# Gate units of a streaming encoder layer: sigmoids and stores put off to later places in the order

## The chip, the core and the metric

The kernel runs on one core of one Trainium2 chip, in one launch. The metric is device time in microseconds, the median of several runs; lower is better. Five engines run their own instruction streams: TensorE (PE, with PEld for its weight loads), VectorE (DVE), ScalarE (ACT), GpSimd (POOL) and SyncE (SP), which here only issues DMAs. An engine works through its own stream in order and waits at an instruction until the data and the buffers that it needs are there.

## The reference

One layer over 1024 frames of width 1024, in float32. What the change touches is the gates: two 1024 x 1024 slices of `w_in` give logits, and their sigmoids scale two mixer branches much later.

```python
h = rmsnorm(x, norm_mix_g[li])
z = h @ w_in[li]
qa, fa, ia, ga, qb, kb, vb, gate_a, gate_b = jnp.split(z, split_at, axis=-1)
...
merged = (jax.nn.sigmoid(gate_a) * (oa @ w_branch_a[li])
          + jax.nn.sigmoid(gate_b) * (ob @ w_branch_b[li]))
x = x + merged @ w_out[li]
```

The rest (the HGRN2 mixer, banded attention, SwiGLU, the per-layer embedding) is as long as the layer but is not edited.

## The kernel before

Activations lie feature-major, 128 partitions by 1024 frames. Each float32 matmul is made of three single-pass ones: both operands are split into a rounded part and a remainder (`whi` and `wlo` for weights), and hi x hi, hi x lo and lo x hi are summed in PSUM. ScalarE makes the rounded part (a CAST), VectorE or GpSimd the remainder.

**Gate units.** 14 of the 16 gate tiles are made in `gate_units` by 7 units, n = 0 to 6, of two output tiles (c = 0, 1) by two halves of the frames. A unit is one Strassen-like step (`strassen`, L1282): 7 products in place of 8, each of 4 chunks of the contraction by 3 matmuls, 12 matmuls of 128x512. From n = 1 on the products run in the order 0 to 6 into three PSUM banks:

- product 0 into b1; ScalarE copies b1 to the tile p1 (the **copy**, `self.A.copy(p1, b1)`)
- product 1 into b2; VectorE adds u2 = p1 + b2
- product 2 into b3
- product 3 on top of b2, which is why it waits for u2; VectorE adds u3 = p1 + b2 + b3, and `done(1, 0, u3)`
- product 4 on top of b1; `done(0, 1, b1)`
- product 5 on top of b2; `done(1, 1, p1 + b2)`
- product 6 on top of b3; u2 += b3 and `done(0, 0, u2)`

Unit 0 (`early`) runs its products in the order 0, 4, 6, 1, 2, 3, 5 and has other places for the four results. `done` is `keep` of `gate_units`: VectorE multiplies the result by the row norms `rb`, ScalarE takes the sigmoid in place, SyncE stores the 256 KB half to DRAM. The result tiles `t` come from a pool of five (`stmp`), so a tile is used again once its store has landed.

**Side work.** `strassen` pulls a generator `side()` after the copy, at five places between the products and at the end. Three things come from it:

- `gate_load`: two weight loads of 512 KB (`wr`) for the next unit. The raw tiles are two, so a load waits until GpSimd has made the last remainders from the old ones.
- `first_weights` (L1077): the next unit's operands from the four quarters of its weights: casts of the first and of the last two quarters with GpSimd's remainders; three **weight sums** by VectorE in place; casts of two sums with VectorE's remainders; a cast and remainder of the third; a last sum, cast and remainder.
- from n = 1 on `quad_item` (L923): a 1 MB load `dq` of weights for a much later product, four **dq sums** by VectorE in place, four stores. It has one buffer, so the next load waits for these stores to land.

**What sets the order.** The code pins the stream of VectorE, ScalarE, GpSimd, TensorE and SyncE to the order in which the Python code emits the instructions (`order`, through `self.V`, `self.A`, `self.G`, `load`, `store`). No scheduler moves them in this stage. Behind the units comes `near(0)`, where GpSimd (L470) makes remainders in tiles that lie where the dq buffer lay, and TensorE multiplies them by `onesr`.

Of the kernel before, what the change touches and what calls it, by code (L numbers as in the profile page):

```python
# [13 lines left out]
AF = mybir.ActivationFunctionType  # L14
# [40 lines left out]
class Trunk:  # L55
# [296 lines left out]
    def gate_units(self, first, then):  # L352

        h0, h1 = slice(0, HALF), slice(HALF, T)
        cut = lambda pair, h: [t[:, h] for t in pair]
        odd, even = self.u[1::2], self.u[0::2]
        self.sops = [
            [cut(p, h1) for p in odd], [cut(a, h1) for a, _ in self.ts], [cut(b, h0) for _, b in self.ts],
            [cut(a, h0) for a, _ in self.ts], [cut(p, h1) for p in even], [cut(b, h1) for _, b in self.ts], [cut(p, h0) for p in even]]
        self.gd = [self.spill() for _ in range(2 * GATES)]  # L360

        for n in range(GATES):
            def keep(c, half, ps):
                hs = slice(half * HALF, half * HALF + HALF)
                t = self.stmp() if n and (c, half) == (0, 1) else ps
                self.V.tensor_tensor(t, ps, self.rb[:, hs], ALU.mult)
                self.A.activation(t, t, AF.Sigmoid)
                self.store(self.gd[2 * n + c][:, hs], t)

            def side():  # L370
                more, item = iter(()), iter(())
                if n + 1 < GATES:
                    self.gate_load()
                    more = self.first_weights()
                else:
                    then()
                if n:
                    item = self.quad_item(1, 0)
                    next(item)
                yield  # L380
                yield
                next(more, None)
                next(more, None)
                yield
                next(item, None)
                next(item, None)
                next(more, None)
                yield
                next(more, None)
                next(item, None)  # L390
                yield
                drain(more)
                drain(item)

            self.strassen(keep, side(), early=n == 0)


    def hgrn_in(self, h, outs=None, first=None):
# [1298 lines left out]
def drain(stream):  # L1697
    while True:
        try:
            next(stream)  # L1700
        except StopIteration as e:
            return e.value
# [114 lines left out]
```

## Time and profile before

| | |
|---|---|
| median of 3 runs | 1654.88 us (1654.5 to 1656.84) |
| span of the profiled execution | 1655.2 us |
| PE busy | 1597.5 us, 97% |
| DVE busy | 1190.9 us, 72% |
| POOL busy | 702.9 us, 42% |
| ACT busy | 618.6 us, 37% |
| DMA, mean over the span | 123 GB/s |
| mean granted TensorE clock | 0.985 |

Busy shares are means over stages with different limits. The gate units lie between about 75 and 230 us of the span. In a timeline row stand the start, the duration, the engine, the line, the operation, the tiles written and read (without their numbers), the shape, and in brackets how long the engine had been idle and who ended that. Nearly all rows of this stage bear the line of a helper that records the order (L52, L76, L81), so they are told apart by their tiles: `pm` is a PSUM bank, `t` a result tile, `wr` raw weights, `d` a DRAM tile. Rows of SPq are DMA issues; where several are merged, the duration runs from the first to the last.

### The profile page before, as it was taken

The numbers are of one execution on the slowest core, as the hardware profiler recorded it, in microseconds if no ns is written. First come the engines' busy times: TensorE is split into PE (matmuls) and PEld (weight loads), VectorE is DVE, ScalarE is ACT, GpSimd is POOL, SyncE is SP. The second block draws the span as 40 slices with busy tenths as digits, with TensorE's granted clock in tenths as the row PEclk, the third lists the DMA queues.
The fourth block names the chain that finished last, engine by engine and source line by source line (L and its number), as shares of the span: only waits on it lengthen the run. The fifth ranks groups of instructions, "written<-read, shape, count | busy, mean of one in ns | idle before, by whom it ended". The sixth has DMA issues, their size and how long they took to land.

```text
span 1655.2 us, 22544 instructions
## 1 busy us (share of the span) xinstructions
PE 1597.5 (97%) x8656; PEld 1351.9 (82%) x8656; DVE 1190.9 (72%) x1838; ACT 618.6 (37%) x1080; POOL 702.9 (42%) x408
## 2 busy tenths in 40 slices
PE   6988889999999999999898999999999999999998
PEld 5876769898989999878686788888888888888887
DVE  8755667676648888756988798888888866446653
ACT  5422232122117777631365532222222234435421
POOL 2222342232134322213523377777776665545420
PEclk9999999999999999999999999999999999999999
DMA  4025551211010110087534432233332268655521
GB/s 184 27 101 191 197 184 65 89 39 47 30 62 16 43 43 35 14 317 273 197 127 165 148 101 96 95 104 100 110 113 96 70 220 317 220 190 185 197 76 52
DMA packets 70524, 204.36 MB, mean 123 GB/s; under 512 B 7952, under 2 KB 8720, under 8 KB 68496
## 3 DMA queue, kind: packets, MB, share of 16 engines
q1 hardware_dynamic: 70272, 202.90, 35.0%
q8 instruction: 68, 1.11, 0.3%
q14 instruction: 40, 0.33, 0.1%
q10 hardware_dynamic: 144, 0.02, 0.0%
HBM read 147.05 MB, written 55.84 MB: 123 GB/s over the span
## 4 chain that ended last, share of the span: by engine, by line
PE 43%; DVE 5%; DMA 1%; ACT 1%; issue 1%; POOL 1%; SPq 0%; DVEq 0%; ACTq 0%
PE pm L81 43%; DVE s L52 4%; ACT s L52 1%; POOL wl L124 1%; DMA wr<-in_sg 0%; DMA wr<-d 0%; DMA wr<-in_su 0%; DVE q L52 0%; DMA wr<-in_pp 0%; ACT wh L121 0%; DVE wl L124 0%; ACT q L52 0%; ACT whi L52 0%; DVE wr L52 0%; POOL s L840 0%
## 5 line engine op out<-in xcount | busy, mean ns | idle before, releaser
L81 PE MATMUL pm<-s,wh 128*128 128x512 f32 (+1 forms) x1688 | 525.3, 392 | 16.6 <-DVE s L52 10.7
L81 PE MATMUL pm<-s,whi 128*128 128x512 f32 x1568 | 494.6, 397 | 9.1 <-ACT whi L52 3.5
L124 POOL TENSOR_TENSOR wl<-wr,wh 128x1024 fp32r<-128x1024 f32 (+2 forms) x100 | 251.6, 2521 | 367.6 <-ACT wh L121 362.0
L81 PEld LDWEIGHTS pm<-s,wh 128*128 128x128 f32 x1688 | 316.3, 189 | 84.1 <-DVE s L52 12.9
L81 PEld LDWEIGHTS pm<-s,whi 128*128 128x128 f32 x1568 | 298.2, 190 | 78.3 <-ACT whi L52 3.9
L81 PE MATMUL pm<-s,wl 128*128 128x512 f32 (+1 forms) x844 | 329.4, 390 | 0.0
L81 PE MATMUL pm<-s,wlo 128*128 128x512 f32 x784 | 310.4, 396 | 0.0
L52 DVE TENSOR_TENSOR s<-s,s 128x512 f32<-128x512 f32 (+3 forms) x202 | 251.0, 1269 | 75.2 <-ACT s L52 41.6
L81 PE MATMUL pm<-wh,s 128*128 128x256 f32 (+1 forms) x1152 | 252.3, 304 | 0.1
L121 ACT CAST wh<-wr 128x1024 fp32r<-128x1024 f32 (+2 forms) x106 | 106.4, 1005 | 292.8 <-PE pm L81 126.2
L52 POOL TENSOR_TENSOR wlo<-wr,whi 128x512 fp32r<-128x512 f32 x74 | 139.1, 1889 | 149.7 <-ACT whi L52 149.0
L81 PEld LDWEIGHTS pm<-wh,s 128*128 128x128 f32 x1152 | 191.5, 192 | 5.5 <-DVE s L52 0.3
L81 PEld LDWEIGHTS pm<-s,wl 128*128 128x128 f32 x844 | 159.7, 189 | 33.0 <-POOL wl L124 0.5
L81 PEld LDWEIGHTS pm<-s,wlo 128*128 128x128 f32 x784 | 149.1, 190 | 34.3 <-DVE wlo L52 0.5
L81 PE MATMUL pm<-wl,s 128*128 128x256 f32 (+1 forms) x576 | 170.6, 296 | 0.0
L52 DVE TENSOR_TENSOR t<-pm,t 128x512 f32<-128x512 f32 x143 | 98.2, 687 | 86.5 <-PE pm L81 76.0
L52 POOL TENSOR_TENSOR s<-s,t 128x512 f32<-128x512 f32 x44 | 76.5, 1739 | 90.0 <-ACT t L52 90.0
L81 PEld LDWEIGHTS pm<-wl,s 128*128 128x128 f32 x576 | 111.0, 193 | 2.1
L52 DVE TENSOR_TENSOR s<-pm,s 128x512 f32<-128x512 f32 x101 | 65.3, 684 | 61.9 <-PE pm L81 61.9
L52 ACT CAST whi<-q 128x512 fp32r<-128x512 f32 (+1 forms) x63 | 47.8, 759 | 156.5 <-DVE q L52 134.5
L81 PE MATMUL pm<-s,s 128*128 128x64 f32 (+4 forms) x776 | 98.3, 267 | 1.9 <-DVE s L52 1.7
L81 PEld LDWEIGHTS pm<-s,s 128*128 128x128 f32 (+2 forms) x776 | 86.5, 174 | 7.4 <-DVE s L52 3.6
(141 smaller groups left out, 1940.8 us busy)
## 6 DMA issues: line engine op xcount, KB each, us to landing
s<-d SPq DMA_DIRECT2D x65, 512.0 KB, 5.9
d<-s SPq DMA_DIRECT2D x87, 256.0 KB, 2.8
d<-dq SPq DMA_DIRECT2D x60, 256.0 KB, 2.6
wr<-d SPq DMA_DIRECT2D x28, 512.0 KB, 3.7
dq<-in_wq SPq DMA_DIRECT2D x11, 1024.0 KB, 7.7
wr<-in_sg SPq DMA_DIRECT2D x22, 512.0 KB, 3.9
wr<-in_su SPq DMA_DIRECT2D x22, 512.0 KB, 4.3
d<-t SPq DMA_DIRECT2D x34, 256.0 KB, 2.1
```

Source lines behind the costliest of these rows:

```text
L52: return lambda *a, **k: self.trunk.order(op(*a, **k), self.key)
L81: return self.order(self.nc.tensor.matmul(*a, **k))
L121: self.nc.scalar.copy(hi[:, c], raw[:, c])
L124: rest.tensor_tensor(lo[:, c], raw[:, c], f32(hi[:, c]), ALU.subtract)
```

## The change

`keep` no longer emits the sigmoid and the store; it puts them on a list. `flush` emits what is on the list, and is called in `side()` after the copy (behind the issue of the weight loads), after product 3 and after product 4 once the weight steps are emitted, and behind the last unit. The dq sums are pulled one by one, the last at the end of the unit, and so are the four dq stores. The number of instructions of each kind does not change, and TensorE's order stays.

```diff
--- before.py
+++ after.py
@@ -359,13 +359,20 @@
             [cut(a, h0) for a, _ in self.ts], [cut(p, h1) for p in even], [cut(b, h1) for _, b in self.ts], [cut(p, h0) for p in even]]
         self.gd = [self.spill() for _ in range(2 * GATES)]
 
+        late = []
+
+        def flush():
+            while late:
+                t, c, hs = late.pop(0)
+                self.A.activation(t, t, AF.Sigmoid)
+                self.store(self.gd[c][:, hs], t)
+
         for n in range(GATES):
             def keep(c, half, ps):
                 hs = slice(half * HALF, half * HALF + HALF)
                 t = self.stmp() if n and (c, half) == (0, 1) else ps
                 self.V.tensor_tensor(t, ps, self.rb[:, hs], ALU.mult)
-                self.A.activation(t, t, AF.Sigmoid)
-                self.store(self.gd[2 * n + c][:, hs], t)
+                late.append((t, 2 * n + c, hs))
 
             def side():
                 more, item = iter(()), iter(())
@@ -374,6 +381,7 @@
                     more = self.first_weights()
                 else:
                     then()
+                flush()
                 if n:
                     item = self.quad_item(1, 0)
                     next(item)
@@ -382,10 +390,15 @@
                 next(more, None)
                 next(more, None)
                 yield
+                next(more, None)
+                flush()
                 next(item, None)
+                yield
+                next(more, None)
+                flush()
                 next(item, None)
+                yield
                 next(more, None)
-                yield
                 next(more, None)
                 next(item, None)
                 yield
@@ -393,6 +406,7 @@
                 drain(item)
 
             self.strassen(keep, side(), early=n == 0)
+        flush()
 
 
     def hgrn_in(self, h, outs=None, first=None):
```

Three places of the order follow, without what stays. Numbers tell tiles apart and differ between the two programs.

ScalarE in unit 0, before: `COPY` is the copy, `t_754`, `t_808`, `t_779` are results, `whi` casts of weights.

```order
L52 COPY t_722<-pm_707 128x512
L52 ACTIVATE t_754<-t_754 128x512
L52 CAST whi_759<-wr_724 128x512
L52 CAST whi_761<-wr_726 128x1024
L52 ACTIVATE t_808<-t_808 128x512
L52 ACTIVATE t_779<-t_779 128x512
```

The same place now:

```order
L52 COPY t_722<-pm_707 128x512
L52 CAST whi_757<-wr_724 128x512
L52 CAST whi_759<-wr_726 128x1024
L52 ACTIVATE t_754<-t_754 128x512
L52 CAST whi_815<-wr_724 128x512
L52 CAST whi_815<-wr_726 128x512
```

The casts of the first and last quarters now stand ahead of the first sigmoid, and those of the weight sums ahead of the second and third.

ScalarE from the weight loads of unit 2 to the copy of unit 3, before (`t_1074`, `t_1097`, `t_1120`, `t_1040` are the four results in the order of the products, the `COPY` is unit 3's):

```order
L52 CAST whi_1054<-wr_1022 128x512
L52 CAST whi_1056<-wr_1024 128x1024
L52 ACTIVATE t_1074<-t_1074 128x512
L52 ACTIVATE t_1097<-t_1097 128x512
L52 CAST whi_1101<-wr_1022 128x512
L52 CAST whi_1101<-wr_1024 128x512
L52 ACTIVATE t_1120<-t_1120 128x512
L52 CAST whi_1125<-wr_1022 128x512
L52 CAST whi_1130<-wr_1024 128x512
L52 ACTIVATE t_1040<-t_1040 128x512
L52 COPY t_1170<-pm_1155 128x512
```

And now (`t_1074`, `t_1096`, `t_1119`, `t_1040`):

```order
L52 CAST whi_1054<-wr_1018 128x512
L52 CAST whi_1056<-wr_1020 128x1024
L52 ACTIVATE t_1074<-t_1074 128x512
L52 CAST whi_1098<-wr_1018 128x512
L52 CAST whi_1098<-wr_1020 128x512
L52 ACTIVATE t_1096<-t_1096 128x512
L52 CAST whi_1122<-wr_1018 128x512
L52 CAST whi_1127<-wr_1020 128x512
L52 COPY t_1166<-pm_1151 128x512
L52 ACTIVATE t_1119<-t_1119 128x512
L52 ACTIVATE t_1040<-t_1040 128x512
```

The copy now stands ahead of the last two sigmoids of the unit before it.

VectorE in the same unit, from behind the scaling of the first result, before (`dq` rows are dq sums, `wr` rows weight sums, `wlo` remainders):

```order
L52 TENSOR_TENSOR dq_1026<-dq_1026 128x512 x2
L52 TENSOR_TENSOR wr_1024<-wr_1022,wr_1024 128x512
L52 TENSOR_TENSOR wr_1022<-wr_1022 128x512
L52 TENSOR_TENSOR wr_1022<-wr_1024,wr_1022 128x512
L52 TENSOR_TENSOR t_1097<-pm_1005,rb_447 128x512
L52 TENSOR_TENSOR wlo_1102<-wr_1022,whi_1101 128x512
L52 TENSOR_TENSOR wlo_1102<-wr_1024,whi_1101 128x512
L52 TENSOR_TENSOR dq_1026<-dq_1026 128x512
L52 TENSOR_TENSOR t_1120<-pm_1006,t_1020 128x512
L52 TENSOR_TENSOR t_1120<-t_1120,rb_447 128x512
L52 TENSOR_TENSOR wr_1024<-wr_1024,wr_1022 128x512
L52 TENSOR_TENSOR dq_1026<-dq_1026 128x512
```

And now:

```order
L52 TENSOR_TENSOR wr_1020<-wr_1018,wr_1020 128x512
L52 TENSOR_TENSOR wr_1018<-wr_1018 128x512
L52 TENSOR_TENSOR wr_1018<-wr_1020,wr_1018 128x512
L52 TENSOR_TENSOR dq_1026<-dq_1026 128x512
L52 TENSOR_TENSOR t_1096<-pm_1001,rb_447 128x512
L52 TENSOR_TENSOR wlo_1099<-wr_1018,whi_1098 128x512
L52 TENSOR_TENSOR wlo_1099<-wr_1020,whi_1098 128x512
L52 TENSOR_TENSOR dq_1026<-dq_1026 128x512
L52 TENSOR_TENSOR t_1119<-pm_1002,t_1016 128x512
L52 TENSOR_TENSOR t_1119<-t_1119,rb_447 128x512
L52 TENSOR_TENSOR wr_1020<-wr_1020,wr_1018 128x512
L52 TENSOR_TENSOR dq_1026<-dq_1026 128x512
```

Behind these rows both have two rows on `t_1040`, the last result; the changed kernel has one more dq sum behind them. So the first two dq sums went from ahead of the weight sums to behind them (the second behind the remainders), and the last went behind the last result.

SyncE from the first result's store of unit 2 to the dq load of unit 3, before (`d<-t` is a store of a sigmoid, `d<-dq` a dq store, `wr` and `dq` loads):

```order
L76 DMA d_698<-t_1074 128x512
L76 DMA d_697<-t_1097 128x512
L76 DMA d_698<-t_1120 128x512
L76 DMA d_981<-dq_1026 128x512
L76 DMA d_983<-dq_1026 128x512
L76 DMA d_985<-dq_1026 128x512
L76 DMA d_987<-dq_1026 128x512
L76 DMA d_697<-t_1040 128x512
L76 DMA wr_1172<-in_gs 128x1024
L76 DMA wr_1174<-in_gs 128x1024
L76 DMA dq_1176<-in_oq 128x2048
```

And now:

```order
L76 DMA d_698<-t_1074 128x512
L76 DMA d_697<-t_1096 128x512
L76 DMA d_993<-dq_1026 128x512
L76 DMA d_995<-dq_1026 128x512
L76 DMA d_997<-dq_1026 128x512
L76 DMA d_999<-dq_1026 128x512
L76 DMA wr_1168<-in_gs 128x1024
L76 DMA wr_1170<-in_gs 128x1024
L76 DMA d_698<-t_1119 128x512
L76 DMA d_697<-t_1040 128x512
L76 DMA dq_1176<-in_oq 128x2048
```

The last two sigmoid stores went behind the next unit's two weight loads, so that these now stand right behind the four dq stores.

## The prediction

> **What bounds the kernel now.** The page's first part gives TensorE 97% of the span, so time can only be won where TensorE stands still. I looked for that in the table of stretches, cut at the starts of the gate units: columns are the stretch, its length, busy time of TensorE, weight loads, VectorE, ScalarE and GpSimd with counts, the granted clock, the DMA share and GB/s.
>
> ```profile
> 97.00:116.50 19.50, 19.50 (x85) 15.85 (x84) 9.87 (x14) 4.46 (x7) 6.41 (x4) 0.99 0.40 141
> ...
> 160.30:184.66 24.36, 21.79 (x85) 16.69 (x84) 15.71 (x22) 6.73 (x11) 6.74 (x4) 0.93 0.51 173
> ```
>
> Unit 1 (first row) runs through in 19.5 us: seven products of 2.79 us. Unit 4 takes 24.4. The waits of TensorE between 97 and 230 us say on whom, and the timeline gives the first and the last of the five waits (units 2 to 6):
>
> ```profile
> PE pm L81 <- DVE t L52: 9.7, 5, 2.2
> ...
> 126.34 0.73 PE L81 MATMUL pm<-tl,whi 128*128 128x512 f32 x2 [1.33 <-DVE t L52]
> ...
> 218.35 0.74 PE L81 MATMUL pm<-tl,whi 128*128 128x512 f32 x2 [1.65 <-DVE t L52]
> ```
>
> Each is the start of the unit's fourth product, p3. It adds into the bank that VectorE has first to read (u2 = copy of p0 + p1). Four turns in 218.35 - 126.34 = 92.0 us are 23.0 us a turn, 3.5 more than TensorE needs. So something else turns round in 23 us. The timeline of unit 3 shows it, from the loads after its copy to the next unit's p3:
>
> ```profile
> 148.35 0.90 SPq L76 DMA_DIRECT2D wr<-in_gs  x2
> 149.85 0.33 SPq L76 DMA_DIRECT2D dq<-in_oq  x1
> ...
> 154.92 1.05 ACT L52 CAST whi<-wr 128x1024 fp32r<-128x1024 f32 x1 [0.46 <-DMA wr<-in_gs]
> 156.05 2.41 POOL L52 TENSOR_TENSOR wlo<-wr,whi 128x1024 fp32r<-128x1024 f32 x1 [0.21 <-ACT whi L52]
> 157.42 2.31 DVE L52 TENSOR_TENSOR dq<-dq 128x512 f32<-128x512 f32 x2 [3.03 <-DMA dq<-in_oq]
> 159.64 0.68 DVE L52 TENSOR_TENSOR wr<-wr,wr 128x512 f32<-128x512 f32 x1
> 161.70 0.68 DVE L52 TENSOR_TENSOR t<-pm,rb 128x512 f32<-128x512 f32 x1
> 163.63 1.29 DVE L52 TENSOR_TENSOR wlo<-wr,whi 128x512 fp32r<-128x512 f32 x2 [1.25 <-ACT whi L52]
> ...
> 168.02 1.97 SPq L76 DMA_DIRECT2D d<-dq  x4
> 168.70 1.30 DVE L52 TENSOR_TENSOR t<-t,rb 128x512 f32<-128x512 f32 x1
> 170.03 0.63 ACT L52 ACTIVATE t<-t 128x512 f32<-128x512 f32 x1 [1.43 <-DVE t L52]
> 170.57 0.57 ACT L52 COPY t<-pm 128x512 f32<-128x512 f32 x1
> 170.69 0.32 SPq L76 DMA_DIRECT2D d<-t  x1
> 171.10 0.95 SPq L76 DMA_DIRECT2D wr<-in_gs  x2
> 171.17 0.69 DVE L52 TENSOR_TENSOR t<-pm,t 128x512 f32<-128x512 f32 x1 [1.17 <-ACT t L52]
> 171.91 0.84 PE L81 MATMUL pm<-tl,whi 128*128 128x512 f32 x2 [2.21 <-DVE t L52]
> ...
> 178.37 1.05 ACT L52 CAST whi<-wr 128x1024 fp32r<-128x1024 f32 x1 [0.57 <-DMA wr<-in_gs]
> ```
>
> Read it as a **ring**. SyncE issues weight and dq loads; VectorE stands 3.03 us until dq lands and does two dq sums ahead of the weight sums (159.64), the casts, the remainders and the last tile's scaling (168.70). Only then can ScalarE make the last sigmoid (170.03), behind it the copy, and SyncE that sigmoid's store (170.69), behind which the next loads wait. Once round: 171.10 - 148.35 = 22.75 us. The copy's own input was ready long before: p3 was due 2.2 us ahead of 171.91 and stands two products (5.6) behind p0, which so ended near 164.
>
> **The change part by part.** (1) In units 2 to 6 the copy no longer stands behind two sigmoids, nor the loads behind their stores. (2) The two dq sums ahead of the weight sums go behind them, the last dq sum behind the last scaling, and its store (S4) stands on SyncE just ahead of the next loads. No instruction is added or removed; durations stay, places change. So the sum is a new ring, and I cost it from the end of the last dq sum (D) to the next D:
>
> - S4's issue: 1.97 / 4 = 0.5 us.
> - First weight load to the cast of the second: 154.92 - 148.35 = 6.6 us now, 178.4 - 171.1 = 7.3 in the next unit. I take 6.2, since three of the four dq stores will have left earlier and the dq load, which waits for S4 to land (2.6 us, below), comes 2.2 us behind the first weight load in place of 1.5. Ends: 3.6, the shortest issue to landing of any such load here, and 7.7 (unit 1, below).
> - Cast and remainder: 1.1 + 2.4 = 3.5 us; VectorE's weight sums wait for the latter.
> - First weight sum to D: now 159.64 to 170.00 (end of the scaling) is 10.4. Between the sums and the remainders there is an idle 1.25 now, because the casts wait behind a sigmoid; one dq sum (0.6) fits in that gap, and the casts go ahead of the sigmoid, so this piece shrinks from 4.0 to 3.3. Behind the scaling comes a dq sum, 0.7. One more operation falls beside GpSimd and takes 1.3 in place of 0.7, as at 168.70: I add 0.5. Sum 10.8, ends 10.3 and 11.4.
>
> The landings (of the dq stores the median; of the weight loads least, median, most):
>
> ```profile
> d<-dq SPq DMA_DIRECT2D x24, 256.0 KB, 2.6
> ...
> DMA to landing us min/median/max: 3.6/5.8/6.8
> ```
>
> **Ring after: 0.5 + 6.2 + 3.5 + 10.8 = 21.0 us**, with ends 17.9 (then TensorE's 19.5 rules) and 23.1. The dq load makes a shorter ring: 0.5 + 2.6 + 7.6 of load (149.85 to 157.42) reach 10.7 behind D, and its sum is due 0.5 + 6.2 + 3.5 + 2.1 = 12.3 behind D. So the 3.03 us wait goes, and the weight pair is next late. What is hidden: the copy at 3.1 us into a unit has ScalarE free; the late sigmoids and their two stores pass behind it while VectorE waits for p3, and the tiles those stores hold are wanted again only at p4 and p5, over 10 us later. If that cover failed, VectorE would wait there for a store of some 2 us.
>
> (3) Unit 0 has another order of products: ScalarE gave its first sigmoid, which waits for VectorE, ahead of two weight casts.
>
> ```profile
> 81.88 0.59 ACT L52 COPY t<-pm 128x512 f32<-128x512 f32 x1 [2.27 <-DVE s L52]
> 83.95 0.63 ACT L52 ACTIVATE t<-t 128x512 f32<-128x512 f32 x1 [1.49 <-DVE t L52]
> 84.49 1.55 ACT L52 CAST whi<-wr 128x512 fp32r<-128x512 f32 x2
> 85.17 3.62 POOL L52 TENSOR_TENSOR wlo<-wr,whi 128x512 fp32r<-128x512 f32 x2 [15.86 <-ACT whi L52]
> 88.83 0.69 DVE L52 TENSOR_TENSOR wr<-wr,wr 128x512 f32<-128x512 f32 x1 [4.31 <-POOL wlo L52]
> 91.63 1.22 PE L81 MATMUL pm<-tl,whi 128*128 128x512 f32 x2 [4.00 <-DVE t L52]
> ```
>
> The casts can follow the copy at 82.47, 2.0 us earlier; GpSimd, the weight sums and TensorE's last product follow: it starts at 89.6, and unit 1 at 92.4. Behind this gap TensorE ran at half clock:
>
> ```profile
> 91.60:97.00 5.40, 5.37 (x13) 4.21 (x14) 4.08 (x7) 2.29 (x4) 0.00 (x0) 0.50 0.20 77
> 149.00:155.00 6.00, 5.86 (x25) 4.80 (x26) 2.16 (x4) 0.70 (x2) 0.46 (x1) 1.00 1.03 303
> 173.00:175.00 2.00, 2.00 (x6) 1.61 (x5) 0.00 (x0) 0.00 (x0) 0.00 (x0) 0.50 0.92 176
> ```
>
> The gap left is 2.1 us. One of that length cost the clock at 173 (0.50), another did not at 149 (1.00): I charge half of the 1.0 us by which a slow last product would hold up VectorE. The Trainium skill, "TensorE: Matmul & The Clock Gate", Part 1, has the clock halved after at least one idle window of about 3.4 us; by it this gap costs nothing and the forecast would be 0.5 us lower, but the row at 173, behind 2.21 us, speaks against it.
>
> First ring: unit 1's loads and cast now stand at
>
> ```profile
> 101.48 1.58 SPq L76 DMA_DIRECT2D wr<-in_gs  x2
> ...
> 109.15 1.05 ACT L52 CAST whi<-wr 128x1024 fp32r<-128x1024 f32 x1 [3.29 <-DMA wr<-in_gs]
> ```
>
> or 7.7 us apart. The last product of unit 0, 89.6, lets VectorE finish the old weights at 96.2, and the first load leaves then. Cast at 103.9, sums at 107.5, D1 = 118.3. p3 of unit 2 can start at 92.4 + 19.5 + 8.4 = 120.2: no stall. After that D grows by 21.0 a turn: D5 = 118.3 + 84.0 = 202.3, and 0.7 later, at 203.0, unit 6 starts p3: **15.35 us before 218.35**.
>
> (4) Behind the last unit:
>
> ```profile
> 226.65 3.43 DVE L52 TENSOR_TENSOR dq<-dq 128x512 f32<-128x512 f32 x2 [3.06 <-DMA dq<-in_wq]
> 233.76 1.96 SPq L76 DMA_DIRECT2D d<-dq  x4
> 238.46 4.05 POOL L470 TENSOR_TENSOR m<-m,m 128x512 fp32r<-128x512 f32 x3 [9.66 <-DMA d<-dq]
> 240.11 0.80 PE L81 MATMUL pm<-m,onesr 128*128 128x512 f32 x2 [2.66 <-POOL m L470]
> ```
>
> GpSimd starts there 20.1 us behind p3, on the landing of the dq stores. After: D5 is 0.7 ahead of p3, and 0.5 + 2.6 + 7.6 later dq lands, 10.0 behind p3; nine operations of VectorE, 0.6 to 0.7 each (no weight sums here), end the last dq sum at 16.0, and 0.5 + 2.6 later S4 has landed, 19.1 behind p3: 1.0 us gained. Whether the gain lasts is read behind the stage:
>
> ```profile
> 275.00:300.00 25.00, 25.00 (x211) 24.87 (x211) 17.12 (x39) 8.10 (x16) 8.11 (x5) 1.00 0.01 2
> ```
>
> TensorE is full there at full clock, and no load is awaited: an earlier start stays earlier.
>
> **Sum:** 15.35 + 1.0 - 0.5 = 15.85 us. The profiled span is 1655.2, so 1639.35; the median of the runs (1654.88) is 0.3 lower, hence **1639.0 us**.
>
> **The rivals.** With ring L, p3 of unit 6 starts at 119.0 + 4 L, but not before 120.2 + 4 x 19.5 = 198.2.
>
> - *TensorE rules.* If the weight pair lands in 4.7 us or less (3.6 has been seen for one load), L is under 19.5: 20.15 + 1.0 = 21.15 us, 1633.7. For it: the queue ahead of the pair is emptier. The Trainium skill, "DMA: Bandwidth & Descriptors", under "Two DMAs through the same engine are not ordered", says that descriptors of one queue start in order, so a dq load behind the pair should not hold it up. Against it: unit 1's pair took 7.7 us with little ahead and a dq load behind.
> - *The ring stays.* S4 replaces the sigmoid's store as what the loads wait for, contention eats the rest, L = 22.8: p3 at 210.2, 8.15 + 1.0 = 9.15 us, 1645.7.
> - *The gain is lost later*, in the stretch after 240 us where GpSimd and VectorE already hold TensorE up: 1654.9. Against it is the full row at 275.
> - *Slower.* The loads queue behind S4, and S4 behind everything VectorE does in a unit. Each us that the pair then takes longer costs 4. Nothing is gained at L = 25.1; above L = 25.9, a pair in 11.1 us, it is slower by over 3.3. L = 27 gives 1662.5. The longest pair here is 7.7.
>
> **How the numbers follow.** Forecast (L 20.3 to 21.8) 0.50; TensorE rules 0.18; ring stays 0.18; lost later 0.09; slower 0.05. 0.2% (3.3 us) is about what a measurement of this kernel can tell from no change. Faster: the first three, 0.86; same 0.09; slower 0.05. The range takes in the first three with about 2 us on each side for the clock and the tail: 1632 to 1648.
>
> **What would show it.** Right: p5 of unit 0 near 89.6; the copy about 3.1 us into each unit, before both sigmoids; no VectorE wait on a dq load in units 2 to 5; p3 of unit 6 near 203 with waits of about 1.5 us in units 3 to 6, still on VectorE. Wrong, if the turns are 22.8 us or more with VectorE waiting for GpSimd's remainder and that for a weight load; if a unit waits on a store of a sigmoid; or if unit 6 is 15 us earlier and the span is not.

## The result, and the profile after

| | before | after |
|---|---|---|
| median | 1654.69 us (1652.26 to 1656.84, 4 runs) | 1638.84 us (1637.78 to 1640.24, 4 runs) |
| ratio, 95% interval | | 0.9908 (0.9891 to 0.9924) |
| span of the profiled execution | 1655.2 us | 1638.5 us |
| mean granted TensorE clock | 0.985 | 0.991 |
| turn of the ring in units 2 to 6 | 23.0 us | 21.4 us |

Timed again later, beside another kernel, the changed kernel took 1640.32 us (1638.5 to 1643.86, 6 runs; ratio 0.9921, 0.9904 to 0.9937). It is faster by 14 to 16 us, with 15.85 forecast.

The timeline of the changed kernel from unit 2's weight loads to unit 3's p3, rows of all engines, with the columns as before:

```profile
117.84 0.88 SPq L76 DMA_DIRECT2D wr<-in_gs  x2
118.81 0.86 SPq L76 DMA_DIRECT2D d<-t  x2
119.83 0.85 SPq L76 DMA_DIRECT2D dq<-in_oq  x1
124.49 1.05 ACT L52 CAST whi<-wr 128x1024 fp32r<-128x1024 f32 x1 [0.63 <-DMA wr<-in_gs]
128.05 0.69 DVE L52 TENSOR_TENSOR wr<-wr,wr 128x512 f32<-128x512 f32 x1 [4.26 <-POOL wlo L52]
135.62 0.62 ACT L52 CAST whi<-wr 128x512 fp32r<-128x512 f32 x1 [2.99 <-DVE wr L52]
136.14 0.58 ACT L52 COPY t<-pm 128x512 f32<-128x512 f32 x1
136.74 1.42 DVE L52 TENSOR_TENSOR t<-t,rb 128x512 f32<-128x512 f32 x1
138.09 0.68 DVE L52 TENSOR_TENSOR dq<-dq 128x512 f32<-128x512 f32 x1
139.21 0.89 SPq L76 DMA_DIRECT2D wr<-in_gs  x2
139.42 0.73 PE L81 MATMUL pm<-tl,whi 128*128 128x512 f32 x2 [1.19 <-DVE t L52]
```

The order is the one forecast. The copy (136.14) comes ahead of the last scaling (136.74), and so of the last sigmoid; it has just waited for the unit's last cast (135.62), which waits for VectorE's last weight sum. VectorE no longer waits for dq; it waits 4.26 us for GpSimd's remainder of the second weight load. The next loads (139.21) leave 0.44 us behind D, the end of the last dq sum at 138.77. One turn, from D = 117.40 to 138.77, is 0.44 + 6.65 (first load to second cast, 117.84 to 124.49) + 3.56 (to 128.05) + 10.72 (to 138.77) = 21.37 us. The forecast had 0.5 + 6.2 + 3.5 + 10.8 = 21.0. **Only the pair's term is off by more than 0.1.** The two sigmoid stores at 118.81 went right behind the pair, and the experiments come back to them.

The waits of TensorE between 97 and 230 us, and the last of them in the timeline (unit 6):

```profile
PE pm L81 <- DVE t L52: 6.3, 4, 1.8
...
203.54 0.73 PE L81 MATMUL pm<-tl,whi 128*128 128x512 f32 x2 [1.63 <-DVE t L52]
```

9.7 us in five waits became 6.3 in four: unit 2 starts its p3 without one. p3 of unit 6 starts at 203.54, 14.81 earlier than 218.35.

Unit 0 (product order of its own), and the first gap of TensorE behind the last unit:

```profile
79.97 0.58 ACT L52 COPY t<-pm 128x512 f32<-128x512 f32 x1 [2.27 <-DVE s L52]
80.45 1.57 ACT L52 CAST whi<-wr 128x512 fp32r<-128x512 f32 x2
81.15 4.08 POOL L52 TENSOR_TENSOR wlo<-wr,whi 128x512 fp32r<-128x512 f32 x2 [13.74 <-ACT whi L52]
81.31 1.68 DVE L52 TENSOR_TENSOR t<-t,rb 128x512 f32<-128x512 f32 x1
88.07 0.73 PE L81 MATMUL pm<-tl,whi 128*128 128x512 f32 x2 [1.37 <-DVE t L52]
...
223.96 0.73 PE L81 MATMUL pm<-m,onesr 128*128 128x512 f32 x2 [1.33 <-POOL m L484]
```

The copy of unit 0 starts 1.91 us earlier than before (81.88), though nothing ahead of it was changed. In the profiles of all kernels of this study it starts between 79.5 and 82.0, with no tie to the edit: this part of the profiles' difference is chance. From here on, places are counted from that copy. The last product of unit 0 comes 8.10 us behind it, was 9.75: 1.65 us won, where 2.03 were forecast. The casts do follow the copy at once, but now a scaling of VectorE falls beside GpSimd's remainders, and both are longer (1.68 us; 4.08 where it was 3.62).

### The profile page after: what moved, and what is told of

The parts are those of the page before. It is cut to its first block, busy times and chain, and to the rows that moved or that the text cites. A ratio compares the mean times of both kernels' runs of the same rounds, so it can differ in the third digit from the quotient of the medians.

```text
span 1638.5 us, 22553 instructions
## 1 busy us (share of the span) xinstructions
PE 1590.3 (97%) x8656; PEld 1348.1 (82%) x8656; DVE 1191.1 (73%) x1838; ACT 618.3 (38%) x1080; POOL 702.1 (43%) x408
## 4 chain that ended last, share of the span: by engine, by line
PE 44%; DVE 6%; DMA 1%; ACT 1%; issue 1%; POOL 0%; SPq 0%; DVEq 0%; ACTq 0%
PE pm L81 44%; DVE s L52 5%; DMA wr<-in_sg 1%; DVE wl L124 1%; ACT s L52 1%; DMA wr<-in_su 0%; DMA wr<-d 0%; DVE q L52 0%; ACT whi L52 0%; DVE pl L52 0%; DVE wr L52 0%; ACT wh L121 0%; POOL s L854 0%; SPq L76 0%; ACT q L52 0%
## 5 line engine op out<-in xcount | busy, mean ns | idle before, releaser
L52 ACT CAST whi<-wr 128x512 fp32r<-128x512 f32 x90 | 67.2, 757 | 86.1 <-DVE wr L52 49.7
```

Source lines behind the costliest of these rows:

```text
L52: return lambda *a, **k: self.trunk.order(op(*a, **k), self.key)
```

## The experiments

All times are medians; "u0 to u6" is the way from unit 0's copy to unit 6's copy in the profile (217.00 - 81.88 before), which leaves the start-up and the work behind the units out. Each ratio is to runs of the kernel before that were timed beside that kernel.

| kernel | us (range, runs) | ratio to before, 95% | u0 to u6, us |
|---|---|---|---|
| before | 1654.69 (1652.26 to 1656.84, 4) | | 135.12 |
| the change | 1638.84 (1637.78 to 1640.24, 4) | 0.9908 (0.9891 to 0.9924) | 120.29 |
| e1 late sigmoids only | 1636.68 (1631.36 to 1637.74, 6) | 0.988 (0.986 to 0.9901) | 117.13 |
| e2 dq order only | 1662.64 (1660.19 to 1665.92, 8) | 1.0047 (1.0031 to 1.0063) | 139.64 |
| e3 unit 0 as before | 1643.86 (1639.2 to 1653.37, 12) | 0.9945 (0.9926 to 0.9963) | 122.98 |
| e4 dq stores behind loads | 1644.43 (1643.69 to 1645.38, 6) | 0.9935 (0.9918 to 0.9953) | 121.05 |
| e5 dq load late | 1655.57 (1650.59 to 1656.58, 8) | 1.0002 (0.9989 to 1.0015) | 125.82 |
| e6 last dq sum first | 1630.99 (1628.45 to 1635.63, 5) | 0.9866 (0.9845 to 0.9887) | 113.42 |
| e7 copy first only | 1645.74 (1641.4 to 1655.47, 12) | 0.9954 (0.9934 to 0.9974) | 127.03 |
| e8 casts first only | 1644.61 (1643.31 to 1646.31, 6) | 0.9943 (0.9927 to 0.9958) | 124.71 |
| e9 stores late too | 1655.81 (1651.45 to 1658.83, 8) | 1.0002 (0.9986 to 1.0018) | 125.83 |

Of all edits below, the lines are against the changed kernel unless another is named.

### Which half of the change opens the ring

e1 keeps the late sigmoids and puts the dq sums back ahead of the weight sums:

```diff
                 yield
-                next(more, None)
-                flush()
                 next(item, None)
-                yield
+                next(item, None)
                 next(more, None)
                 flush()
-                next(item, None)
                 yield
                 next(more, None)
-                next(more, None)
+                flush()
                 next(item, None)
                 yield
```

> Late sigmoids and stores as in the changed kernel; dq sums and weight sums in their old places. Changed kernel: 1638.8 us, unit 6's p3 at 123.57 us behind unit 0's copy, a turn 21.3; kernel before: 1654.7, 136.47, 23.0. Theory A (either half opens the ring): the loads no longer stand behind the last sigmoid; dq's own loop is then the longest: store issue 0.5, landing 2.6, load to first dq sum 7.6, from there to the last dq sum 9.4 to 10.6, so 20.1 to 21.3 a turn and a time of 1636 to 1641, with a VectorE wait on the dq load still there. Theory B (the halves only work together): the dq wait of some 3 us stays ahead of the weight sums, the turn stays near 22.8 and the time is 1648 to 1653.

e2 keeps the new order of dq sums, weight sums and casts, and emits each sigmoid at once:

```diff
                 late.append((t, 2 * n + c, hs))
+                flush()
```

> dq sums, weight sums and casts in the new order; each sigmoid and its store emitted at once, as before (unit 0 too). Theory A: the next loads wait for S4, which leaves about as late as the last sigmoid's store, so the turn is still 21.3; the copy behind the last sigmoid makes p3 about 0.6 later in each unit but not more each turn; unit 0 loses its 1.65 us and up to 1 us more by a lower clock. Together 1641 to 1643.5, no VectorE wait on dq in units 2 to 5. Theory B: the copy behind the sigmoids closes the old ring; turn 22.8, 1648 to 1653.

Theory A held for e1: 1636.7 us, as fast as the whole change or a little faster. One turn in its timeline, from last dq sum to last dq sum:

```profile
134.99 0.68 DVE L52 TENSOR_TENSOR dq<-dq 128x512 f32<-128x512 f32 x1
136.11 1.42 SPq L76 DMA_DIRECT2D wr<-in_gs  x2
139.31 0.33 SPq L76 DMA_DIRECT2D dq<-in_oq  x1
146.77 1.42 DVE L52 TENSOR_TENSOR dq<-dq 128x512 f32<-128x512 f32 x2 [2.58 <-DMA d<-t]
148.11 0.68 DVE L52 TENSOR_TENSOR wr<-wr,wr 128x512 f32<-128x512 f32 x1
155.06 0.68 DVE L52 TENSOR_TENSOR dq<-dq 128x512 f32<-128x512 f32 x1
```

The ring now closes over dq: from D' (the last dq sum's end, 135.67) 3.64 to the dq load, 7.46 to the first dq sum, 1.34 to the weight sums, 7.63 to the next D': 20.07 us. Between the copies of units 2 to 6 a turn takes 20.0 to 21.3. Its wait is still there (2.58; the row names a store, but dq had been issued 7.5 us before). The turn is shorter than the whole change's 21.4, since the last dq sum and S4 stand ahead of the last scaling.

e2 went against both theories: **the dq order alone made the kernel slower**, by 8 us. Its timeline:

```profile
147.44 1.75 DVE L52 TENSOR_TENSOR dq<-dq 128x512 f32<-128x512 f32 x1
150.72 1.25 SPq L76 DMA_DIRECT2D wr<-in_gs  x2
157.22 1.05 ACT L52 CAST whi<-wr 128x1024 fp32r<-128x1024 f32 x1 [0.53 <-DMA wr<-in_gs]
160.78 0.69 DVE L52 TENSOR_TENSOR wr<-wr,wr 128x512 f32<-128x512 f32 x1 [4.20 <-POOL wlo L52]
165.39 1.29 DVE L52 TENSOR_TENSOR wlo<-wr,whi 128x512 fp32r<-128x512 f32 x2 [1.26 <-ACT whi L52]
169.91 2.96 POOL L52 TENSOR_TENSOR wlo<-wr,whi 128x512 fp32r<-128x512 f32 x2 [9.16 <-ACT whi L52]
171.67 1.75 DVE L52 TENSOR_TENSOR dq<-dq 128x512 f32<-128x512 f32 x1
```

From D = 149.19 it is 1.53 to the loads, 6.50, 3.56 and 12.64 to D = 173.42: 24.2 us a turn. The pair costs no more than in the changed kernel (6.65). Two other terms grew. The casts stand behind a sigmoid again, so VectorE idles 1.26 ahead of its remainders; GpSimd's last remainders (169.91) come late and lie beside the last dq sum, which takes 1.75 in place of 0.68; together 12.64 in place of 10.72. And the four dq stores, held up behind a sigmoid's store, leave one behind the other, 1.53 in place of 0.44. My expectation had costed neither.

e7 and e8 split e1 further. In units 1 to 6 of e7 only the last two sigmoids are late, in e8 only the first two:

```diff
                 late.append((t, 2 * n + c, hs))
+                if n and (c, half) in ((1, 0), (0, 1)):
+                    flush()
```

This is e7, against e1. In e8 the pairs are `((1, 1), (0, 0))`.

> Late sigmoids with dq and weight sums in the old places, but in units 1 to 6 only the last two sigmoids and stores of a unit come behind the next copy and the next loads; the first two stand where they stood before, ahead of two casts. Theory A: VectorE's idle 1.25 us between the weight sums and their remainders is back (0.8 us more from the first weight sum to the last dq sum, 8.4 in place of 7.6), turn 20.9 in place of 20.1: 1639 to 1641. Theory B (the casts matter more than the copy): 1646 or more. Theory C (the casts are free): 1636 to 1637.5.

> The other half: in units 1 to 6 the first two sigmoids come late, behind the casts, but the last two stand ahead of the copy and their stores ahead of the next loads, as before. Theory A: the loads wait for the last sigmoid's store, 2.8 us behind S4's issue (scaling 2.0, sigmoid 0.6, store and copy the rest), turn 20.1 + 2.3 to 2.8 = 22.4 to 22.9: 1648 to 1652. Theory B (the casts are the gain): 1641 or less.

Both came out 8 to 9 us slower than e1. e7 just misses the 1646 of its Theory B and lies well above Theory A, though its runs scatter over 14 us; e8 lost less than its Theory A said. e7's VectorE, behind the weight sums:

```profile
157.97 1.29 DVE L52 TENSOR_TENSOR wlo<-wr,whi 128x512 fp32r<-128x512 f32 x2 [1.25 <-ACT whi L52]
159.18 1.78 DVE L52 TENSOR_TENSOR dq<-dq 128x512 f32<-128x512 f32 x1
```

The idle 1.25 is back, as expected, and behind it a dq sum of 1.78 beside GpSimd, which was not: copies stand 22.4 us apart (141.10 to 163.53), 2.4 more than in e1. e8, from the last dq sum:

```profile
136.66 0.69 DVE L52 TENSOR_TENSOR dq<-dq 128x512 f32<-128x512 f32 x1
139.97 0.32 SPq L76 DMA_DIRECT2D d<-t  x1
140.41 0.91 SPq L76 DMA_DIRECT2D wr<-in_gs  x2
141.92 0.33 SPq L76 DMA_DIRECT2D dq<-in_oq  x1
149.67 2.31 DVE L52 TENSOR_TENSOR dq<-dq 128x512 f32<-128x512 f32 x2 [3.24 <-DMA dq<-in_oq]
```

The loads wait for the last sigmoid's store and leave 3.06 us behind the last dq sum, not 0.44. Only 1.7 us reach the turn (21.8, copies at 139.85 and 161.66), since the ring runs over dq: its load leaves 4.57 behind D' (e1 3.64), and its two sums take 2.3 beside GpSimd (e1 1.4). The copy is late in e8 too (VectorE waits 1.17 us for it), but this ring does not run through it. From unit 1's copy to unit 6's, e7 loses 2.0 us a turn against e1 and e8 1.5: the casts ahead of the first sigmoids and the loads ahead of the last stores are each worth that much, and only with both does e1 come near TensorE's 19.5.

### Unit 0

e3 flushes at once in unit 0 alone:

```diff
                 late.append((t, 2 * n + c, hs))
+                if n == 0:
+                    flush()
```

> The changed kernel, but in unit 0 alone each sigmoid stands ahead of the casts again. Theory A: unit 0's last product starts 1.65 us later (9.75 us behind unit 0's copy, not 8.1), the first ring starts from there, and the 1.65 us stay to the end, with 0.5 to 1 us more for a product at half clock: 1640.5 to 1641.5. Theory B: the first load of unit 1 waits for something else, and the start of unit 0's last product is no term of the sum: 1638.5 to 1639.3.

```profile
89.29 1.22 PE L81 MATMUL pm<-tl,whi 128*128 128x512 f32 x2 [4.00 <-DVE t L52]
...
89.30:95.00 5.70, 5.70 (x18) 4.54 (x19) 4.39 (x7) 2.29 (x4) 0.00 (x0) 0.73 0.24 92
```

The first row (timeline) has the last product 9.76 us behind the copy at 79.53, the wait of 4.00 us back; the second (table of stretches, clock third from the end) the lower clock behind it. u0 to u6 is 2.69 longer than in the changed kernel, which is Theory A: 1.65, and 1.0 for the clock. The median says 5 us, more than either theory, but this kernel's runs, like e7's, scatter over 14 us; why, I did not find.

### What is left of the ring

e4 (first diff, at the head and the end of `side`) puts the dq stores behind the next unit's weight loads; e6 (second, behind p5) puts the last dq sum and the stores ahead of the last scaling:

```diff
+                while rest:
+                    drain(rest.pop(0))
                 flush()
                 if n:
-                    item = self.quad_item(1, 0)
+                    item = self.quad_item(1, 1)
+                    rest.append(item)
...
                 drain(more)
-                drain(item)
+                next(item, None)
```

```diff
                 next(more, None)
                 next(more, None)
                 next(item, None)
+                next(item, None)
                 yield
```

> The changed kernel, with the four stores of the dq sums on SyncE behind the next unit's two weight loads. Theory A (the ring is closed by S4 ahead of the loads): the loads can leave 1.5 to 4 us earlier, when the old raw tiles are read, the ring falls under 19.5, and TensorE rules: its waits of 1.19, 1.81, 1.64 and 1.63 us in units 3 to 6 go, time 1632 to 1633.5. Theory B (the DMA queue is the limit): the pair takes longer by what it starts earlier, turn 20.5 or more, 1636 to 1639. Theory C (slower): the dq load waits for the stores, VectorE waits for dq again, 1640 or more.

> The changed kernel with one step moved: the last dq sum and the stores stand ahead of the unit's last scaling on VectorE, no longer behind it. Theory A (the ring of the changed kernel runs through the last scaling because S4 stands ahead of the next loads): from the first weight sum to S4's sum 8.7 us in place of 10.7, ring 0.5 + 6.65 + 3.56 + 8.7 = 19.4, under TensorE's 19.5; TensorE's waits of 6.3 us in units 3 to 6 nearly vanish, unit 6's copy at 116.5 to 118 us behind unit 0's (123.6 less 3.3 is 120.3 in the changed kernel), time 1632 to 1635. Theory B (earlier loads only land slower, or dq is then late): the turn stays over 20.8, 1637 or more.

e4 followed Theory C. Its timeline:

```profile
138.08 2.39 SPq L76 DMA_DIRECT2D wr<-in_gs  x2
140.52 2.48 SPq L76 DMA_DIRECT2D d<-dq  x4
148.41 0.33 SPq L76 DMA_DIRECT2D dq<-in_oq  x1
149.45 0.69 DVE L52 TENSOR_TENSOR wr<-wr,wr 128x512 f32<-128x512 f32 x1 [2.30 <-POOL wlo L52]
153.75 0.69 DVE L52 TENSOR_TENSOR dq<-dq 128x512 f32<-128x512 f32 x1 [2.15 <-DMA dq<-in_oq]
161.73 0.68 DVE L52 TENSOR_TENSOR dq<-dq 128x512 f32<-128x512 f32 x1
```

The weights did come earlier: the loads leave 3.2 us ahead of D (141.26), the weight sums start 8.2 behind it (changed kernel: 10.65). But the stores behind the pair land later, the dq load waits for them until 7.15 us behind D (was 2.4 to 2.8), and its sum is now late by 2.15. The ring passes over dq: 7.15 + 5.34 + 8.66 = 21.15. One load was freed by holding up the other. u0 to u6 is 0.8 longer than in the changed kernel; the rest of the 5.6 us between the medians lies behind the units and was not taken apart.

e6 did what Theory A said, and more:

```profile
PEld pm L81 <- DVE t L52: 0.4, 1, 0.4
...
156.55 1.08 SPq L76 DMA_DIRECT2D wr<-in_gs  x2
163.40 1.05 ACT L52 CAST whi<-wr 128x1024 fp32r<-128x1024 f32 x1 [0.57 <-DMA wr<-in_gs]
```

The first row is all that the waits show of TensorE's two queues between 92 and 215 us; the matmul queue waits for nobody. The copies come 19.5 to 19.7 us apart, which is TensorE's own pace. The pair still takes 6.85 (156.55 to 163.40); what went is the last scaling and the sum behind it between the weight sums and S4. To rule out the chip, the changed kernel and e6 ran again side by side:

> The changed kernel again, on the chip of the next one and timed beside it: 1637 to 1641 us; unit 6's copy 120.3 us behind unit 0's, within 0.3, since the ring has no term of chance; the time from the start of the span to unit 0's copy, which has run from 79.5 to 82.0 us in ten kernels without regard to the edit, may be anywhere in there.

> The changed kernel with the last dq sum and the dq stores ahead of the last scaling, again, beside the changed kernel on one chip. Theory A (S4 behind the last scaling is what is left of the ring): faster than the changed kernel by the 6.3 us that TensorE waited, 5 to 8 us, at 1631 to 1634. Theory B (the difference seen before came from the chip): within 2 us of the changed kernel.

1640.32 us (1638.5 to 1643.86, 6 runs) against 1631.6 (1630.14 to 1634.2, 4 runs), ratios to before 0.9921 (0.9904 to 0.9937) and 0.9865 (0.9843 to 0.9886); u0 to u6 120.41 and 113.26. **e6 beats both kernels**, by 8.7 us here and by 23 against before. Some 2 us more came than the waits held; part of that lies behind the units, where it was not taken apart.

### Why the weight pair takes 6.65 us

In e5 the dq load is issued from the place of the first late sigmoid, behind its store, so that the pair has landed by then. In e9 the stores of the last two sigmoids wait there too:

```diff
                 flush()
-                if n:
-                    item = self.quad_item(1, 0)
-                    next(item)
                 yield
...
                 next(more, None)
                 flush()
-                next(item, None)
+                if n:
+                    item = self.quad_item(1, 0)
+                    next(item)
                 yield
```

e9, against e5; the flush at the head of `side` is called with `keep` set:

```diff
+        late, kept = [], []
...
         def flush(keep=False):
             while late:
                 t, c, hs = late.pop(0)
                 self.A.activation(t, t, AF.Sigmoid)
-                self.store(self.gd[c][:, hs], t)
+                kept.append((t, c, hs))
+            while kept and not keep:
+                t, c, hs = kept.pop()
+                self.store(self.gd[c][:, hs], t)
```

> The changed kernel with the dq load issued behind the store of the unit's first late sigmoid, some 6 us later, when the weight pair has landed; the dq sums go one place later each. Read is only the time from the first weight load's issue to the cast of the second, 6.65 us in units 2 to 5 of the changed kernel. Theory A (the dq load behind the pair shares the transfer engines with it and stretches it): 5.0 to 5.8 us. Theory B (transfers of a queue are served in their order, so what is behind does not matter): 6.4 to 6.8 us.

> As in the kernel with the dq load issued late, and also the stores of a unit's last two sigmoids issued only behind the casts of the next weight pair, so that SyncE has nothing behind the pair until it has landed; S4 alone is ahead of it. Read is only the time from the first weight load's issue to the cast of the second (6.65 us in the changed kernel, 6.6 to 6.7, once 7.3, with the dq load late). Theory A (the sigmoids' stores share the transfer engines with the pair): 5.0 to 6.1 us. Theory B (the pair's own megabyte and the S4 ahead of it take this long): 6.4 to 6.8 us.

Both are slow kernels, at the time of the one before, as the dq sums are late in them; only the pair is read. The timelines of e5 and then of e9:

```profile
120.87 0.90 SPq L76 DMA_DIRECT2D wr<-in_gs  x2
127.53 1.05 ACT L52 CAST whi<-wr 128x1024 fp32r<-128x1024 f32 x1 [0.55 <-DMA wr<-in_gs]
129.56 0.37 SPq L76 DMA_DIRECT2D dq<-in_oq  x1
```

```profile
121.04 0.90 SPq L76 DMA_DIRECT2D wr<-in_gs  x2
126.93 1.06 ACT L52 CAST whi<-wr 128x1024 fp32r<-128x1024 f32 x1 [0.55 <-DMA wr<-in_gs]
128.99 1.31 SPq L76 DMA_DIRECT2D d<-t  x3
```

Without the dq load the pair took 6.66, 6.67, 7.33 and 6.60 us in units 2 to 5; the changed kernel has 6.65, 6.76, 6.64 and 6.58. The two are not quite alike, since in e5 the third dq store leaves only 1.1 us ahead of the pair, in the changed kernel 3.1. In e6 it leaves as late as in e5, and there, with the dq load behind, the pair took 6.60, 6.89, 6.85 and 6.78. So, unit by unit, the dq load behind the pair costs it about 0.2 us at most there. Without the two stores as well (e9) it took 5.89, 5.89, 6.21 and 5.80. **The two sigmoid stores, 0.5 MB issued right behind the pair, stretch it by about 0.8 us** (0.77 to 1.12 between e5 and e9, which differ in nothing else near the pair).

Unit 1 has no dq store ahead of its pair. There the pair took 7.48 us in the changed kernel (7.55 when it ran again; 7.49 and 7.26 in e6's two runs), 7.08 without the dq load and 6.37 without the sigmoid store as well, so in that place the dq load does cost some 0.2 to 0.5 us.

The Trainium skill, "DMA: Bandwidth & Descriptors", under "Two DMAs through the same engine are not ordered", says that descriptors of one queue start in order but are pipelined, with reads and writes apart. Read alone, its first half would let nothing behind the pair delay it: units 2 to 5 of e5 nearly agree for the dq load, and e9's 0.8 us for the stores does not. The second half leaves room for that.

## Why the prediction was right, and where it was not

- **What bounds the kernel** (VectorE's and SyncE's ring around the weight pair, not TensorE): right. e6 takes the ring's last surplus away and the waits at p3 are gone.
- **What carries the gain.** I listed two parts and costed one ring for both. e1 and e2 show that the parts are not of a kind: late sigmoids alone bring the whole gain, the new dq order alone loses 8 us, and beside the late sigmoids it gives away some 3 us of the ring again (u0 to u6: 117.13 against 120.29), because it puts the last dq sum, and with it S4 and the loads, behind the last scaling. The ring of the whole change was costed right; its halves I could not have told.
- **The step that was mis-sized: the weight pair**, 6.2 forecast, 6.65 measured. I argued that three of the four dq stores would have left and the dq load would come later. Both happened, and by e5 and e6 the dq load mattered little. What I left out are the two sigmoid stores: under "what is hidden" I let them pass behind the copy at no cost, but they now stand right behind the pair, and e9 puts about 0.8 us a turn on them.
- **Other terms:** S4's issue 0.44 (0.5), cast and remainder 3.56 (3.5), first weight sum to D 10.72 (10.8). Turn 21.37 where 21.0 was forecast: 1.5 us over four turns.
- **The copy** was to come about 3.1 us into each unit. In units 3 to 6 it comes 6.3 to 6.9 us in, since on ScalarE it still stands behind the last weight cast. That cost nothing: in unit 3 the copy ended at 136.72, and VectorE, which p3 waits for, ended its last dq sum only at 138.77.
- **Unit 0:** 1.65 us in place of 2.03, since GpSimd's remainders now share their time with a scaling (4.08 and 1.68 us). The first ring's end D1 stood 37.4 us behind the copy, not 36.4: 0.4 of this 1.0 is the late last product, the rest lies between it and the first load. The gap left at the last product is 1.37 us, not 2.1, as the product ahead of it now waits 1.37 in place of 0.38. No half clock followed, so the 0.5 charged for it was not due.
- **The dq wait** went, as forecast, in units 2 to 5, and the pair became what VectorE waits for. With the dq stores moved (e4) the dq load leaves 4.7 us later and dq is late again, by 2.15.
- **The tail:** 1.34 us gained between p3 of unit 6 and the first gap behind it (223.96 for 240.11, less 14.81), 1.0 forecast; 0.8 when the changed kernel ran again.
- **The sum** came nearer than its terms, and that is luck. The profiles differ by 16.7: 1.91 by a start-up that had nothing to do with the change, 12.9 where 15.35 was forecast, 1.34 in the tail, and some 0.5 of clock and rest. The medians differ by 15.85, the very number forecast, and by 14.3 in the second comparison. The 2.4 us by which the gate units fell short are about the scatter of the runs; only the trace shows them.
- **The rivals.** "TensorE rules" needed a pair under 4.7 us; even with nothing behind it the pair takes 5.8 to 6.2. It was reached in e6 by another way. "The ring stays" is what e2 comes to, and worse; "slower" did happen there too, though by VectorE's and ScalarE's order, not by a longer pair. "Lost later" is refuted by the changed kernel's end.

## What to carry to other kernels

When a ring closes over several engines, write it as a sum of terms between two passes of one instruction, and take for each edit the term that it changes: here one reordering shortened two terms and another, in the same diff, lengthened one, which only running the halves apart showed. A store put off to leave the path still uses the queue where it lands; look at which load it now stands beside. And before a load is made to wait for the last of several stores, see whether that store's producer can go a few instructions earlier, which was worth 8.7 us here for one added line.

## What had not been expected of the hardware

- VectorE and GpSimd hold each other up where both read two SBUF tiles. A dq sum or a scaling takes 0.68 us alone; in units 2 to 5 it mostly took 1.06 to 1.78 where a remainder of GpSimd was already running. Where VectorE started first it kept its 0.68 and GpSimd's operation grew: in the changed kernel the dq sum at 132.52 took 0.68 and the remainder from 132.70 took 1.66, 1.30 alone. In unit 0 two remainders took 3.62 us before and 4.08 after. Such a meeting added 1.1 us to one dq sum of each turn in e2 and e7.
- The clock's answer to gaps. The changed kernel's table of stretches behind unit 0 and behind the last unit, and the last gap there (timeline):

```profile
88.00:94.00 6.00, 5.93 (x26) 4.84 (x27) 5.83 (x10) 2.36 (x5) 1.23 (x1) 1.00 0.23 87
...
223.90:232.00 8.10, 5.46 (x26) 4.17 (x26) 7.58 (x7) 2.72 (x3) 8.10 (x5) 0.95 0.39 133
232.00:238.00 6.00, 6.00 (x18) 4.94 (x18) 5.42 (x7) 1.04 (x1) 1.84 (x2) 0.50 0.33 113
...
230.31 2.87 PE L81 MATMUL pm<-s,s 128*128 128x64 f32 x16 [1.63 <-DVE s L52]
```

A gap of 1.37 us left the clock at 1.00, and so did those of 1.19 to 1.81 at p3 of units 3 to 6. Behind the last unit TensorE had gaps of 1.33, 0.94 and 1.63 us and was busy 5.46 of 8.10 us; the clock stayed at 1.00 up to 231 and was 0.50 from 232, so it fell only behind the third gap. But such gaps do not always cost it. In e3 they were 1.21, 0.94 and 1.63 us at the same place, and the clock stayed at 1.00; the kernel of e6, with 0.95 and 1.6 us there, had 1.00 behind them in one run and 0.76 in the other. The Trainium skill, "TensorE: Matmul & The Clock Gate", Part 1, gives at least one idle window of about 3.4 us for a halved clock; no single gap here is so long. What else decides it was not tried.
